# Expert weights in runs of 8 KB, experts finished in pairs, and the crowded path eight experts earlier, in a two-block transformer kernel

## The chip, the cores and the metric

The kernel runs on one core of a Trainium2 chip. The metric is the device time of one execution in microseconds. It was 1775.2 us as the median of three runs (1770.57 to 1777.78 us). The program has five engines with queues of their own: PE (TensorE), DVE (VectorE), ACT (ScalarE), POOL (GpSimd) and SP (SyncE, which here does nothing but issue DMAs). PE's weight loads are listed apart as PEld.

## The reference, cut to what matters

One layer of a first block (attention and HGRN mixers, then a mixture of experts), followed by two layers of a second block, over 256 tokens with 1024 features. The change is in the mixture of experts:

```python
def hier_moe(h, w_rg, b_rg, w_re, b_re, w_gate, w_up, w_down):
    t = h.reshape(B * S, D)                              # 256 x 1024
    ...                                                  # router: two of 32 experts per token
    y = jnp.zeros((B * S, D), jnp.float32)
    for e in range(N_EXPERTS):                           # 32
        hid = jax.nn.silu(t @ w_gate[e]) * (t @ w_up[e]) # w_gate, w_up: 1024 x 512
        y = y + ((hid * dense_w[:, e:e + 1]) @ w_down[e]).astype(jnp.float32)   # 512 x 1024
    return y.reshape(B, S, D).astype(h.dtype)

def first_block(x, ...):
    ...
    x = x + merged @ w_out[l]
    h = rmsnorm(x, g_ffn[l])
    x = x + hier_moe(h, ...)
```

All weights are fp32. One expert has 3 x 1024 x 512 x 4 bytes = 6.29 MB, all 32 have 201.3 MB, and each is read once.

## The kernel before, in words

The program is written in three stages, phase A (mixers and router), phase B (experts) and phase C (second block). A scheduler lays out each engine's instructions from the order of the code and of the data. Buffers come from pools with a fixed number of places. An instruction that writes a place waits until the last reader of what lay there is done, and every engine works through its own list in order, SP too.

**Phase A.** `split_w` cuts fp32 weights into a high and a low part (tiles `hi`, written by ACT, and `lo`, written by DVE, 5 places), and each product is three matmuls (lines 148 to 150). The residual x stands in `x_sb`. At the end, `ev_out` adds the output of `w_out` to x in `x_sb`, transposes it, and the router is worked out.

**Phase B.** For each expert at most CAP = 32 tokens are worked on; a path for more is behind a branch. For eight experts at a time `gather` makes the normalised tokens `xg`, feature major, by matmuls of `x_sb` with one-hot rows `OH` (line 831). Then for each expert e:

- `load_expert(e + 3)` issues the DMAs for the expert three ahead: gate and up weights in two halves (tiles `wgu` or `xgu`, two DMAs of 1024 KB each), down weights in two halves (`wdn` or `xdn`, one DMA of 1024 KB each). There are seven places for halves, so half h of the whole sequence takes the place of half h - 7, that is, the halves of three and a half experts are held. Feature 128 k + p is in partition p at place k, so one run of bytes in memory is 2 KB long in the gate and up weights and 4 KB in the down weights.
- PE makes the gate and up products of 32 tokens, four blocks of 128 hidden features side by side in four column groups of the array (line 922). ACT applies silu, DVE multiplies, PE transposes the 128 x 128 result (line 928), DVE copies it out as `hid`.
- PE multiplies it with the down weights (line 935), two halves of 512 features, each in four column groups, one for each quarter of the hidden features; ACT and DVE copy the two halves out as `part`.
- A matmul with `ohT` scatters these rows to the tokens of both token blocks, and sums the four quarters, in four PSUM accumulators `acc` (line 939). `ohT` is made by DVE and two PE transposes (lines 914 to 918).

At e = 24 stands `overflow()`, the path for crowded experts: it counts tokens per expert, all engines read the largest count, and a branch (line 856) skips the body when the count is not above 32. SP meets that branch after the loads of expert 26 and before those of expert 27. The body would write the tile `part` by DMA. After expert 31, DVE adds the accumulators to `x_sb` (line 947).

**Phase C.** Feed-forward sublayers, pooling and attention, with weight loads `fw` in runs of 1 KB (`ffn_w_in`) and 4 KB (`ffn_w_out`). They use the same rings of places as the experts' weights.

Of the kernel before, what the change touches and what calls it, by code (L numbers as in the profile page):

```python
# [37 lines left out]
def shape_constants():  # L38
# [22 lines left out]
    # pooling: trailing mean minus token, [token in, group, token out]; the first 16 tokens, which have  # L61
    # shorter windows, and what the tokens after a block boundary take from before it, apart
# [10 lines left out]
def tile_model(ctx: ExitStack, tc: tile.TileContext, io, out, dbg=None, stop_after=None):  # L73
# [68 lines left out]
    def row_rstd(tb, scr):  # L142
        ss = small(1, "ss")
        lead["act"] = act.activation(out=scr, in_=x_sb[:, tb], func=AF.Square, accum_out=ss)
        return rstd(ss, 1, 1.0 / D)
# [6 lines left out]
    def split_w(spl, w, lo=None):  # L152
        """w [128, a, b] fp32 (a*b <= 1024) as hi + lo"""
        a, b = w.shape[1], w.shape[2]
        hi = v2(spl.tile([P, 1024], F32R, tag="hi", name="hi")[:, :a * b], b)
        if lo is None:
            lo = spl.tile([P, 1024], F32R, tag="lo", name="lo", bufs=5)
        lo = v2(lo[:, :a * b], b)
        lead["hi"] = act.copy(out=hi, in_=w)  # L159
        lead["lo"] = dve.tensor_tensor(out=lo, in0=w, in1=f32(hi), op=ALU.subtract)  # L160
        return hi, lo

    def gemm_nat(spl, hs, w, evac, tag="g", sw=()):
        """out[t, n] = sum_k h[t, k] w[k, n];  hs[tb] = (hi, lo) [128, KT, 128], w a list of parts [128, k, N<=512],
        sw what is split of w's product before w"""
# [17 lines left out]
    def ada_steps(sl, what, new_ev, tag, new_w, nk, eng):  # L183
        """modulation vectors of sublayer sl, as a list of steps: "ab" the shift and the gain
        (1 + scale) * norm_g as feature columns, "gate" the residual gate over all partitions"""
# [4 lines left out]
        def row(c, h, k0):  # L190
            """rows k0 .. of the product of silu(c) with 512 columns, summed over partitions later"""
# [52 lines left out]
        for c, h in rows:  # L244
# [4 lines left out]
            elif last:  # L249
                # the sums of a row have the time of a step to arrive  # L250
# [50 lines left out]
    # first weights ahead of small loads  # L301
# [65 lines left out]
    # grouped-query attention  # L367
# [95 lines left out]
    # per-feature columns  # L463
# [22 lines left out]
    # HGRN projections, feature major  # L486
# [90 lines left out]
            # within chunks  # L577
# [13 lines left out]
            # k_state to token major, chunk outer products  # L591
# [43 lines left out]
    # gates  # L635
# [3 lines left out]
    sp.dma_start(out=br[:, 4:36], in_=io["b_router_expert"][0:1].to_broadcast([P, 32]))  # L639
    for gi, Gt_ in enumerate((GA, GB)):  # L640
# [7 lines left out]
    # branches  # L648
# [31 lines left out]
    dve.tensor_scalar(out=gcol, in0=gcol, scalar1=float(D) ** 0.5, scalar2=None, op0=ALU.mult)  # L680
    lead["wr"] = dve.tensor_tensor(out=wr, in0=wr, in1=gcol[:, :, None].to_broadcast([P, 8, 36]), op=ALU.mult)
# [11 lines left out]
    def first_max(v, n):  # L693
        """one-hot of the first maximum of each row of v [128, n], and the maximum"""
# [7 lines left out]
    def probs(v, mx, n):  # L702
        """exp(v - max) and the reciprocal of its sum"""
# [6 lines left out]
    def router(tb):  # L710
        """expert weights of the tokens of a block, and each token's place among its expert's tokens"""
# [40 lines left out]
    for h in range(2):  # L752
# [4 lines left out]
        def ev_out(tb, o, h=h):  # L757
            xs = x_sb[:, tb, 512 * h:512 * h + 512]
# [6 lines left out]
            act.copy(out=xT, in_=t)  # L765
            for k in range(4):
# [7 lines left out]
    for tb in range(2):  # L774
        dump(f"x1_{tb}", x_sb[:, tb])
# [12 lines left out]
    def load_expert(e):  # L788
        """halves of the weights in 4 + 3 places in turn; the last experts leave px free"""
# [26 lines left out]
    def one_hots(OH, e, i0, i1):  # L816
        """slots of the tokens of experts e + i0 .. e + i1 - 1, times the tokens' norm factors"""
# [5 lines left out]
    def gather(OH, xg, i0, i1):  # L823
        """the normalised tokens of these experts, feature major"""
# [755 lines left out]
```

## Time and profile before

| | |
|---|---|
| time, median of three runs | 1775.2 us |
| lowest and highest | 1770.57, 1777.78 us |
| profiled execution, first to last instruction | 1773.4 us |
| PE busy | 1630.4 us, 92% |
| DVE, ACT busy | 957.4 us (54%), 635.0 us (36%) |
| HBM read | 470.13 MB |
| DMA packets under 2 KB, under 8 KB, in all | 105336, 258808, 258930 |

The profiled execution has no time on record besides its span; the span lies inside the range of the three runs, 1.8 us under their median. A view by stretch lists, for a stretch of the span, each engine's busy time in us with the number of its instructions, the clock granted to TensorE as a share of full speed, the mean busy share of the 16 DMA engines (it can pass 1, since packets overlap), and the GB/s that they moved. A list in order of time gives the start in us, the duration in us, the engine (SPq is SP's queue), the line, the operation, the tiles written and read, and in brackets how long the engine had been idle and what ended that.

### The profile page before, as it was taken

How to read it: one execution, taken by the hardware profiler on the slowest of the kernel's cores; microseconds unless marked ns; L12 is line 12 of the kernel's file. 1: busy time of each engine (PE TensorE's matmuls, PEld its weight loads, DVE VectorE, ACT ScalarE, POOL GpSimd, SP SyncE). 2: the span in 40 equal slices, each digit the busy share in tenths (PEclk: the TensorE clock that was granted, in tenths of full speed). 3: DMA queues.
4: the chain of work that ended last, by engine and by line, in shares of the span. 5: the costliest groups of instructions: out<-in, count | busy, mean ns of one | idle time of the engine just before them, and what ended most of it. 6: DMA issues, size and time to landing. Idle time of an engine off the chain costs nothing.

```text
span 1773.4 us, 25626 instructions
## 1 busy us (share of the span) xinstructions
PE 1630.4 (92%) x10491; PEld 1205.5 (68%) x10491; DVE 957.4 (54%) x1653; ACT 635.0 (36%) x1054; POOL 48.1 (3%) x55
## 2 busy tenths in 40 slices
PE   6999998999888775989999989999999999999998
PEld 5865576434333332337999769997899867789997
DVE  6645664212112110127778666878687777765563
ACT  4754442101001000016434344435543365555341
POOL 3000000000000000000000000000000010000000
PEclk9999898999999887999999989999999999999999
DMA  7476476999999999997998458895798564465540
GB/s 246 157 263 244 166 274 248 336 394 394 393 393 393 394 394 343 393 384 250 322 321 270 135 181 275 286 308 180 257 302 285 177 225 154 155 214 200 181 154 24
DMA packets 258930, 472.90 MB, mean 267 GB/s; under 512 B 12568, under 2 KB 105336, under 8 KB 258808
## 3 DMA queue, kind: packets, MB, share of 16 engines
q1 hardware_dynamic: 258808, 471.21, 75.4%
q8 instruction: 85, 1.39, 0.3%
q14 instruction: 37, 0.30, 0.1%
HBM read 470.13 MB, written 1.05 MB: 266 GB/s over the span
## 4 chain that ended last, share of the span: by engine, by line
PE 53%; DVE 4%; issue 1%; ACT 1%; POOL 1%; DMA 1%; POOLq 0%; SPq 0%; ACTq 0%; DVEq 0%
PE ps_g L150 9%; PE ps_g L148 9%; PE ps_g L149 9%; PE ps_acc L148 5%; PE ps_acc L149 5%; PE ps_acc L150 5%; PE ps_acc L939 2%; PE ps_g L922 2%; PE ps_g L935 1%; POOL rs L137 1%; PE ps_m L1406 1%; PE ps_m L221 1%; DMA fw<-in_ffn_w_in_dram 1%; DVE flo L160 1%; PE ps_m L235 1%
## 5 line engine op out<-in xcount | busy, mean ns | idle before, releaser
L148 PE MATMUL ps_g<-hh,hi 128*128 128x256 f32 x1024 | 293.7, 287 | 0.0
L149 PE MATMUL ps_g<-hl,hi 128*128 128x256 f32 x1024 | 289.9, 283 | 0.0
L150 PE MATMUL ps_g<-hh,fl 128*128 128x256 f32 x1024 | 289.5, 283 | 0.0
L1065 DVE TENSOR_TENSOR fl<-fw,hi 128x1024 fp32r<-128x1024 f32 x176 | 211.4, 1220 | 43.0 <-ACT hi L1064 35.1
L1064 ACT CAST hi<-fw 128x1024 fp32r<-128x1024 f32 x176 | 176.6, 1045 | 118.3 <-PE ps_g L149 76.6
L149 PEld LDWEIGHTS ps_g<-hl,hi 128*128 128x128 f32 x1024 | 194.6, 190 | 3.6 <-issue 2.4
L148 PEld LDWEIGHTS ps_g<-hh,hi 128*128 128x128 f32 x1024 | 193.4, 189 | 2.9 <-issue 1.7
L150 PEld LDWEIGHTS ps_g<-hh,fl 128*128 128x128 f32 x1024 | 193.2, 189 | 0.7 <-issue 0.7
L206 DVE SCALAR_TENSOR_TENSOR ev<-ada,condp,ev 128x512 f32<-128x512 f32 x196 | 146.6, 748 | 4.4 <-DMA ada<-in_ada_w_dram 1.3
L939 PE MATMUL ps_acc<-part,ohT 128*128 128x512 f32 x256 | 122.9, 615 | 24.3 <-ACT part L937 23.7
L150 PE MATMUL ps_acc<-hi,hd 128*128 128x512 f32 x352 | 139.5, 399 | 0.0
L148 PE MATMUL ps_acc<-hi,hd 128*128 128x512 f32 x352 | 138.8, 397 | 0.5 <-ACT hd L1086 0.5
L149 PE MATMUL ps_acc<-fl,hd 128*128 128x512 f32 x352 | 138.7, 395 | 0.0
L160 DVE TENSOR_TENSOR fl<-fw,hi 128x1024 fp32r<-128x1024 f32 x88 | 104.9, 1220 | 19.7 <-ACT hi L159 19.3
L159 ACT CAST hi<-fw 128x1024 fp32r<-128x1024 f32 x88 | 88.6, 1046 | 71.0 <-PE ps_acc L150 69.6
L925 ACT ACTIVATE sg<-ps_g 128x128 f32<-128x128 f32 x32 | 8.9, 277 | 279.8 <-PE ps_g L922 279.8
L939 PEld LDWEIGHTS ps_acc<-part,ohT 128*128 128x128 f32 x256 | 46.0, 193 | 85.7 <-ACT part L937 40.1
L148 PE MATMUL ps_g<-hi,hh 128*128 128x512 f32 x240 | 98.5, 412 | 1.3 <-ACT hh L1010 1.1
L922 PE MATMUL ps_g<-wgu,xg 128*32 128x256 f32 x1280 | 87.7, 396 | 12.3 <-DMA wgu<-in_w_exp_up_dram 12.3
L150 PE MATMUL ps_g<-hi,hl 128*128 128x512 f32 x240 | 97.0, 405 | 0.0
L937 DVE COPY part<-ps_g 128x512 f32<-128x512 f32 x32 | 22.1, 692 | 137.1 <-PE ps_g L935 110.6
L149 PE MATMUL ps_g<-fl,hh 128*128 128x512 f32 x192 | 78.3, 409 | 1.2 <-DVE fl L1065 1.1
(402 smaller groups left out, 2743.2 us busy)
## 6 DMA issues: line engine op xcount, KB each, us to landing
fw<-in_ffn_w_in_dram SPq DMA_DIRECT2D x88, 1024.0 KB, 7.8
ada<-in_ada_w_dram SPq DMA_DIRECT2D x112, 512.0 KB, 5.2
fw<-in_ffn_w_out_dram SPq DMA_DIRECT2D x44, 1024.0 KB, 6.4
wgu<-in_w_exp_gate_dram SPq DMA_DIRECT2D x40, 1024.0 KB
wgu<-in_w_exp_up_dram SPq DMA_DIRECT2D x40, 1024.0 KB, 14.6
wdn<-in_w_exp_down_dram SPq DMA_DIRECT2D x40, 1024.0 KB, 14.1
xgu<-in_w_exp_gate_dram SPq DMA_DIRECT2D x24, 1024.0 KB, 12.9
xgu<-in_w_exp_up_dram SPq DMA_DIRECT2D x24, 1024.0 KB, 14.7
```

Of the source, the lines that this page charges most:

```text
L137: lead["gp"] = gp.tensor_tensor(out=r, in0=ms, in1=mhalf[:, :n], op=ALU.pow)
L148: pe.matmul(o, ah, bh, start=start, stop=False)
L149: pe.matmul(o, ah, bl, start=False, stop=False)
L150: pe.matmul(o, al, bh, start=False, stop=stop)
L159: lead["hi"] = act.copy(out=hi, in_=w)
L160: lead["lo"] = dve.tensor_tensor(out=lo, in0=w, in1=f32(hi), op=ALU.subtract)
L206: eng.scalar_tensor_tensor(out=o, in0=wk, scalar=ck, in1=o, op0=ALU.mult, op1=ALU.add)
L922: pe.matmul(up[32 * j:32 * j + 32], xg[:, k, s0:s0 + CAP], w[k // 4][:, k % 4, :, j * P:j * P + P], start=k == 0, stop=k == 7)
L937: (act.copy if h == 0 else dve.tensor_copy)(out=part[:, 512 * h:512 * h + 512], in_=o)
L939: pe.matmul(acc[tb][h], ohT[:, tb], part[:, 512 * h:512 * h + 512], start=e == 0, stop=e == NE - 1)
L1064: act.copy(out=hi, in_=w[:, k_])
L1065: dve.tensor_tensor(out=lo_[:, k_], in0=w[:, k_], in1=f32(hi), op=ALU.subtract)
```

## The change

Five things are changed together.

1. **Weights.** Feature 8 p + k is now in partition p at place k (4 p + k for the hidden features of the down weights), so each partition's share of a DMA is one run of 8 KB. Gate and up weights of a half stand one behind the other. The tokens' features have to stand in the same order, so `ev_out` writes, by a strided ACT copy, a second form of x, `x_sb`, with feature 8 i + j in column 128 j + i; the plain form is a new tile, `x_in`. The norm gain gets the same order (`gq`). The new tile's room comes from one place fewer for `lo` (4 for 5) and for `w2` (8 for 9).
2. **Pairs.** `up_gate` runs per expert; `down` and the scatter run per pair of experts, after the second one. The four column groups hold two experts with two halves each, and each adds two matmuls in PSUM. One set of scatter matmuls and one `ohT` serve a pair. The number of down matmuls is the same, that of scatter matmuls and of transposes for `ohT` is halved.
3. **Transposes.** The 128 x 128 transpose on PE and its copy become one DVE transpose by 32 x 32 blocks from SBUF to SBUF.
4. **Crowded path.** `overflow()` stands at expert 16.
5. **x.** It is added to the accumulators by four matmuls at expert 26 (`add_x`), and after the last expert ACT and DVE copy two accumulators each to `x_sb`, where DVE had added four.

```diff
-            lo = spl.tile([P, 1024], F32R, tag="lo", name="lo", bufs=5)
+            lo = spl.tile([P, 1024], F32R, tag="lo", name="lo", bufs=4)
...
-    NW2 = 9
+    NW2 = 8
...
         def ev_out(tb, o, h=h):
-            xs = x_sb[:, tb, 512 * h:512 * h + 512]
+            xs = x_in[:, tb, 512 * h:512 * h + 512]
...
             act.copy(out=xT, in_=t)
+            act.copy(out=x_sb[:, tb].rearrange("p (j i) -> p j i", j=8)[:, :, 64 * h:64 * h + 64],
+                     in_=xs.rearrange("p (i j) -> p j i", j=8))
...
-            w = place(q, "gu", 4096, wg).rearrange("p (k a n) -> p k a n", a=2, n=512)
+            w = place(q, "gu", 4096, wg).rearrange("p (a k n) -> p a k n", a=2, n=512)
             for a, nm in enumerate(("w_exp_gate", "w_exp_up")):
-                dst.append((q, w[:, :, a], io[nm][0, e].rearrange("(k p) n -> p k n", p=P)[:, 4 * q:4 * q + 4]))
+                dst.append((q, w[:, a], io[nm][0, e].rearrange("(p k) n -> p k n", k=8)[:, 4 * q:4 * q + 4]))
...
-            dst.append((q + 0.5 if e == 2 else 2, w, io["w_exp_down"][0, e].rearrange("(k p) n -> p k n", p=P)[:, 2 * q:2 * q + 2]))
+            dst.append((q + 0.5 if e == 2 else 2, w, io["w_exp_down"][0, e].rearrange("(p k) n -> p k n", k=4)[:, 2 * q:2 * q + 2]))
...
+    def up_gate(e):
...
+        act.activation(out=sg, in_=up[:, 0], func=AF.Silu)
+        sq = pb.tile([P, P], F32, tag="sq", name="sq", bufs=2)
+        dve.tensor_tensor(out=sq.rearrange("p (j i) -> p i j", j=4), in0=v2(sg, 4), in1=up[:, 1].rearrange("p (i j) -> p i j", j=4), op=ALU.mult)
+        hid = pb.tile([P, P], F32, tag="hid", name="hid", bufs=4)
+        dve.transpose(out=hid, in_=sq)
+        return hid
...
+    def down(e, hid, ohT):
+        wd = [wts.pop(e + i)[1] for i in range(2)]
+        part = pb.tile([P, D], F32, tag="part", name="part", bufs=1)
+        for h in range(2):
+            c_ = slice(512 * h, 512 * h + 512)
+            o = ps("g", 512)
+            for jj in range(2):
+                for i in range(2):
+                    for q in range(2):
+                        r_, j = 32 * (2 * i + q), 2 * q + jj
+                        pe.matmul(o[r_:r_ + 32], hid[i][:, 32 * j:32 * j + 32], wd[i][q][:, jj, c_],
+                                  start=jj == 0, stop=jj == 1)
+            (act.copy if h == 0 else dve.tensor_copy)(out=part[:, c_], in_=o)
+            for tb in range(2):
+                pe.matmul(acc[tb][h], ohT[:, tb], part[:, c_], start=e == 0, stop=e == NE - 2)
...
     for e in range(NE):
-        if e == 24:
+        if e == 16:
             overflow()
+        if e == 26:
+            add_x()
...
+        if e % 2 == 0:
+            hid = [up_gate(e)]
+        else:
+            hid.append(up_gate(e))
+            down(e - 1, hid, back_rows(e - 1))
...
-            dve.tensor_tensor(out=xs, in0=acc[tb][h], in1=xs, op=ALU.add)
+            (dve.tensor_copy if h else act.copy)(out=x_sb[:, tb, 512 * h:512 * h + 512], in_=acc[tb][h])
```

**PE, first two experts.** Before, in PE's list from the end of expert 0's gate and up products (`wgu_2427`) on; `wdn_2428` and `wdn_2429` are expert 0's down weights, `OH` to `128x224` is the gather for experts 1 to 7:

```order
L922 MATMUL ps_g_2570<-wgu_2427,xg_2522 32x256 x16
L928 MATMUL ps_t_2606<-K_65,sg_2603 128x128
L935 MATMUL ps_g_2611<-wdn_2428,hid_2608 32x512 x2
L935 MATMUL ps_g_2611<-wdn_2429,hid_2608 32x512 x2
L935 MATMUL ps_g_2619<-wdn_2428,hid_2608 32x512
L939 MATMUL ps_acc_2518<-part_2610,ohT_2568 128x512
L939 MATMUL ps_acc_2520<-part_2610,ohT_2568 128x512
L935 MATMUL ps_g_2619<-wdn_2428,hid_2608 32x512
L935 MATMUL ps_g_2619<-wdn_2429,hid_2608 32x512 x2
L831 MATMUL ps_g_2641<-OH_2498,x_sb_64 128x224 x3
```

The same place of the changed kernel; `wdn_2436` is now expert 0's first half of the down weights, `wgu_2444` and `wgu_2445` are expert 1's gate and up weights, and L840 is the gather:

```order
L918 MATMUL ps_g_2569<-wgu_2435,xg_2530 32x256 x16
L840 MATMUL ps_g_2622<-OH_2506,x_sb_64 128x224 x4
L840 MATMUL ps_t_2629<-OH_2506,x_sb_64 128x224 x4
L840 MATMUL ps_g_2636<-OH_2506,x_sb_64 128x224 x4
L840 MATMUL ps_t_2643<-OH_2506,x_sb_64 128x224 x4
L918 MATMUL ps_g_2660<-wgu_2444,xg_2530 32x256 x16
L918 MATMUL ps_g_2660<-wgu_2445,xg_2530 32x256 x16
L937 MATMUL ps_t_2699<-K_65,lw_2700 128x128
L937 MATMUL ps_t_2699<-K_65,lw_2704 128x128
L953 MATMUL ps_g_2711<-wdn_2436,hid_2606 32x512
```

The last read of expert 0's down weights has moved behind the gather for experts 1 to 7 and behind expert 1's gate and up products.

**PE, end of the expert stage.** The changed kernel's list from the first read of `wdn_4951` on, the last weights that are loaded (the second half of expert 31's down weights; `wdn_4950` is the first half, `wdn_4865` and `wdn_4866` are expert 30's):

```order
L953 MATMUL ps_g_5170<-wdn_4951,hid_5156 32x512
L953 MATMUL ps_g_5170<-wdn_4865,hid_5117 32x512
L953 MATMUL ps_g_5170<-wdn_4866,hid_5117 32x512
L953 MATMUL ps_g_5170<-wdn_4950,hid_5156 32x512
L953 MATMUL ps_g_5170<-wdn_4951,hid_5156 32x512
L953 MATMUL ps_g_5182<-wdn_4951,hid_5156 32x512
L953 MATMUL ps_g_5182<-wdn_4865,hid_5117 32x512
L957 MATMUL ps_acc_2526<-part_5169,ohT_5167 128x512
L957 MATMUL ps_acc_2528<-part_5169,ohT_5167 128x512
L953 MATMUL ps_g_5182<-wdn_4866,hid_5117 32x512
L953 MATMUL ps_g_5182<-wdn_4950,hid_5156 32x512
L953 MATMUL ps_g_5182<-wdn_4951,hid_5156 32x512
```

Two scatter matmuls follow. Before, eight down matmuls of expert 31 alone stood there with four scatter matmuls behind them; now ten of the pair's sixteen stand behind the read of the last weights to come.

**SP, the branch.** The changed kernel's list of SP around the branch of the crowded path; `wdn_3636` and `wdn_3637` are expert 18's down weights:

```order
L815 DMA wgu_3635<-in_w_exp_gate_dram 128x2048
L815 DMA wgu_3635<-in_w_exp_up_dram 128x2048
L815 DMA wdn_3636<-in_w_exp_down_dram 128x2048
L815 DMA wdn_3637<-in_w_exp_down_dram 128x2048
L864 TENSOR_LOAD cmi_3724
L865 COMPARE_AND_BRANCH
```

Before, the same two rows of the branch (lines 855 and 856) stood behind expert 26's loads. SP's loads keep their order by expert otherwise.

## Rows read from the trace of the kernel before

**Rows 1.** The page: span, and the slices of DMA share and GB/s

```profile
span 1773.4 us, 25626 instructions
...
DMA  7476476999999999997998458895798564465540
GB/s 246 157 263 244 166 274 248 336 394 394 393 393 393 394 394 343 393 384 250 322 321 270 135 181 275 286 308 180 257 302 285 177 225 154 155 214 200 181 154 24
```

**Rows 2.** By stretch: length, PE, PEld, DVE, ACT, POOL busy; clock, DMA share, GB/s

```profile
333.00:688.00 355.00, 290.33 (x2200) 124.96 (x2200) 58.21 (x172) 29.89 (x70) 0.00 (x0) 0.95 1.04 393
688.00:704.00 16.00, 3.75 (x7) 1.22 (x10) 0.00 (x0) 0.58 (x1) 0.00 (x0) 0.50 0.72 257
704.00:781.00 77.00, 70.44 (x554) 26.57 (x553) 13.22 (x36) 5.17 (x12) 0.00 (x0) 1.00 1.04 393
568.00:664.00 96.00, 71.19 (x486) 29.01 (x486) 12.00 (x32) 4.89 (x11) 0.00 (x0) 0.87 1.04 393
```

**Rows 3.** Same columns, three short stretches

```profile
412.00:417.00 5.00, 5.00 (x17) 2.89 (x16) 0.59 (x1) 0.42 (x1) 0.00 (x0) 1.00 1.05 387
403.00:407.00 4.00, 4.00 (x49) 1.91 (x51) 0.00 (x0) 0.00 (x0) 0.00 (x0) 1.00 1.02 408
784.00:793.00 9.00, 7.17 (x85) 3.17 (x78) 1.89 (x5) 0.86 (x2) 0.00 (x0) 1.00 1.10 348
```

**Rows 4.** SP's queue in the expert stage: start, us, line, DMA issued

```profile
319.70 0.37 SPq L806 DMA_DIRECT2D wdn<-in_w_exp_down_dram  x1
...
685.43 1.18 SPq L806 DMA_DIRECT2D xdn<-in_w_exp_down_dram  x1
699.86 0.38 SPq L806 DMA_DIRECT2D xgu<-in_w_exp_gate_dram  x1
...
768.29 2.56 SPq L806 DMA_DIRECT2D wdn<-in_w_exp_down_dram  x2
```

**Rows 5.** PE in the expert stage: start, us, line, operation, idle before it

```profile
345.80 0.33 PE L928 MATMUL ps_t<-K,sg 128*128 128x128 f32 x1 [0.71 <-DVE sg L926]
...
348.34 1.98 PE L939 MATMUL ps_acc<-part,ohT 128*128 128x512 f32 x4
...
358.44 0.33 PE L928 MATMUL ps_t<-K,sg 128*128 128x128 f32 x1 [0.71 <-DVE sg L926]
```

**Rows 6.** PE at the end of the expert stage, same columns

```profile
788.87 1.93 PE L935 MATMUL ps_g<-wdn,hid 128*32 128x512 f32 x16 [0.38 <-DVE hid L930]
791.53 3.70 PE L939 MATMUL ps_acc<-part,ohT 128*128 128x512 f32 x8 [0.72 <-ACT part L937]
...
801.75 0.79 PE L148 MATMUL ps_g<-hi,hh 128*128 128x512 f32 x1 [0.20 <-ACT hi L1064]
```

**Rows 7.** PE at its beginning, same columns

```profile
327.58 1.05 PE L922 MATMUL ps_g<-wgu,xg 128*32 128x256 f32 x10
...
330.08 2.36 PE L922 MATMUL ps_g<-wgu,xg 128*32 128x256 f32 x38
```

**Rows 8.** By stretch (columns of rows 2), two early stretches

```profile
308.00:313.00 5.00, 5.00 (x50) 2.15 (x50) 1.03 (x3) 0.07 (x1) 0.00 (x0) 0.65 0.23 52
330.00:333.00 3.00, 2.44 (x39) 1.19 (x38) 2.22 (x10) 0.28 (x1) 0.00 (x0) 1.00 0.25 44
```

**Rows 9.** What PE waited for, 310 to 842 us: total, times, longest

```profile
PE ps_acc L939 <- ACT part L937: 23.7, 11, 19.6
```

**Rows 10.** Line 856, the branch: durations in ns, first and last start; who waited

```profile
L856 SPq EVENT_SEMAPHORE  x8: 17/17/17, 690.5 to 699.5; - x8
...
  ACT part L937: 22.0, 1
```

**Rows 11.** Tile lo: what its engine sat idle for, and who waited for it

```profile
  PE ps_g L149: 18.0, 16
...
  PE ps_g L149: 1.6, 2
```

**Rows 12.** ACT before the expert stage: a copy of 512 columns

```profile
291.44 0.58 ACT L765 COPY xT<-ps_acc 128x512 f32<-128x512 f32 x1
```

More of the change, by code (lines that the diff above doesn't have):

```diff
@@ L143, in row_rstd @@
         ss = small(1, "ss")
-        lead["act"] = act.activation(out=scr, in_=x_sb[:, tb], func=AF.Square, accum_out=ss)
+        lead["act"] = act.activation(out=scr, in_=x_in[:, tb], func=AF.Square, accum_out=ss)
         return rstd(ss, 1, 1.0 / D)
@@ L639, in tile_model @@
     sp.dma_start(out=br[:, 4:36], in_=io["b_router_expert"][0:1].to_broadcast([P, 32]))
+    sp.dma_start(out=gq, in_=io["g_ffn"][0].rearrange("(p j) -> p j", j=8))
     for gi, Gt_ in enumerate((GA, GB)):
@@ L834, in gather @@
                 k = 2 * q + i
[L835 removed]
+                act.activation(out=xg[:, k, s_], in_=o[:, i], func=AF.Copy, scale=gq[:, k:k + 1])
     OH = new_oh()
@@ L893, in tile_model, with add_x @@
     xg = None
+    def add_x():
+        for tb in range(2):
+            for h in range(2):
+                pe.matmul(acc[tb][h], ident, x_sb[:, tb].rearrange("p (j i) -> p i j", j=8)[:, 64 * h:64 * h + 64],
+                          start=False, stop=False)
+    def up_gate(e):
+        w = wts[e][0]
+        s0 = (e % 8) * CAP
+        up = ps("g", 2, P)
+        for k in range(8):
+            for j in range(4):
+                pe.matmul(up[32 * j:32 * j + 32], xg[:, k, s0:s0 + CAP], w[k // 4][:, :, k % 4, j * P:j * P + P],
+                          start=k == 0, stop=k == 7)
+        sg = pb.tile([P, P], F32, tag="sg", name="sg", bufs=2)
+        act.activation(out=sg, in_=up[:, 0], func=AF.Silu)
[4 more added lines that the diff above has]
+        return hid
@@ new lines, in back_rows @@
+    def back_rows(e):
+        oT_ = ps("t", 2, P)
+        for tb in range(2):
+            lw = pb.tile([P, 2, 2, CAP], F32, tag="lw", name="lw", bufs=2)
+            for i in range(2):
+                dve.tensor_scalar(out=lw[:, i], in0=iota32[:, None, :].to_broadcast([P, 2, CAP]),
+                                  scalar1=posm[:, tb, e + i:e + i + 1], scalar2=dense[:, tb, e + i:e + i + 1],
+                                  op0=ALU.is_equal, op1=ALU.mult)
+            pe.transpose(oT_[:, tb], lw.rearrange("p a b s -> p (a b s)"), ident)
+        ohT = pb.tile([P, 2, P], F32, tag="ohT", name="ohT", bufs=2)
+        dve.tensor_copy(ohT, oT_)
+        return ohT
@@ L908, in tile_model @@
             load_expert(e + 3)
-        w, wd = wts.pop(e)
-        s0 = (e % 8) * CAP
-        oT_ = ps("t", 2, P)
-        for tb in range(2):
-            lw = pb.tile([P, 4, CAP], F32, tag="lw", name="lw", bufs=1)
-            dve.tensor_scalar(out=lw, in0=iota32[:, None, :].to_broadcast([P, 4, CAP]), scalar1=posm[:, tb, e:e + 1],
-                              scalar2=dense[:, tb, e:e + 1], op0=ALU.is_equal, op1=ALU.mult)
-            pe.transpose(oT_[:, tb], lw.rearrange("p a s -> p (a s)"), ident)
-        ohT = pb.tile([P, 2, P], F32, tag="ohT", name="ohT", bufs=2)
-        dve.tensor_copy(ohT, oT_)
-        up = ps("g", 2, P)
-        for k in range(8):
-            for j in range(4):
-                pe.matmul(up[32 * j:32 * j + 32], xg[:, k, s0:s0 + CAP], w[k // 4][:, k % 4, :, j * P:j * P + P],
-                          start=k == 0, stop=k == 7)
-        sg = pb.tile([P, P], F32, tag="sg", name="sg", bufs=2)
-        act.activation(out=sg, in_=up[:, 0], func=AF.Silu)
-        dve.tensor_tensor(out=sg, in0=sg, in1=up[:, 1], op=ALU.mult)
-        hp_ = ps("t", P)
-        pe.transpose(hp_, sg, ident)
-        hid = pb.tile([P, P], F32, tag="hid", name="hid", bufs=2)
-        dve.tensor_copy(hid, hp_)
-        part = pb.tile([P, D], F32, tag="part", name="part", bufs=1)
-        for h in range(2):
-            o = ps("g", 512)
-            for j in range(4):
-                pe.matmul(o[32 * j:32 * j + 32], hid[:, 32 * j:32 * j + 32], wd[j // 2][:, j % 2, 512 * h:512 * h + 512],
-                          start=True, stop=True)
-            (act.copy if h == 0 else dve.tensor_copy)(out=part[:, 512 * h:512 * h + 512], in_=o)
-            for tb in range(2):
-                pe.matmul(acc[tb][h], ohT[:, tb], part[:, 512 * h:512 * h + 512], start=e == 0, stop=e == NE - 1)
+        if e % 2 == 0:
[3 more added lines that the diff above has]
+            down(e - 1, hid, back_rows(e - 1))
         if e == 29:
```

24 lines of the change are left out of this document (14 added, 10 removed).

## The prediction

> **What bounds the kernel now.** I read the slices first. In slices 8 to 18 the DMA share stands at 9 and the rate, in eight of the eleven, at 393 or 394 GB/s [rows 1]: the expert stage, in which 201.3 MB of weights pass. Nowhere else is the rate so flat, and it is the only part in which the change removes much. By stretch, 333 to 688 us ran at 393 GB/s with PE busy 290 of 355 us, and 704 to 781 us at 393 again [rows 2]. Between them lies a hole: 257 GB/s over 16 us, 5.5 us of transfer time lost. So the transfers set the pace, but not all the way to the end. In PE's list one expert takes 358.44 - 345.80 = 12.64 us [rows 5], where its weights take 6.29 MB / 393 GB/s = 16.0 us. Yet from 704 us PE was busy 70 of 77 us at full clock [rows 2]. The reason is the branch. PE waited up to 19.6 us there for ACT's copy into part [rows 9], and ACT 22.0 us for SP at line 856 [rows 10]: the skipped body writes part by DMA, so the copy has to wait until SP is past it. SP came late to the branch, since its last load before it was issued only at 685.43 us, and needed until 699.86 us for the next [rows 4]. After that PE had a backlog that it could not work off in the seven experts left, so its last scatter ended at 791.53 + 3.70 = 795.2 us [rows 6], about 13.7 us after the experts' last bytes (near 781.5 us: at 784 the rate is that of the next stage's loads, 348 GB/s [rows 3]). Both chains must get shorter for the stage to end earlier.
>
> **Transfer rate.** The rows give the price of a run at three lengths. SP's loads go out in order, so a stretch can be matched to its loads: 2 KB runs (gate, up) moved at 387 GB/s, 4 KB runs (down) at 408, 1 KB runs (feed-forward, first stage) at 348 [rows 3]. On one of 16 DMA engines that is 84.7, 160.6 and 47.1 ns a run. One KB more costs 37.6 ns from 1 to 2 KB and 37.9 from 2 to 4 KB: a straight line with about 9.3 ns fixed per run. For 8 KB it gives 160.6 + 4 x 37.9 = 312 ns, an estimate of 420 GB/s. Lower bound: 8 KB no better than 4 KB, 408. Upper: no fixed cost at all, 434. I take 420, since three lengths lie on the line.
>
> From 333 us on, 355 x 393 + 16 x 257 + 77 x 393 = 173.9 MB passed. At 393 GB/s they take 442.5 us, at 420 414.0: **-28.5 us**.
>
> The Trainium skill ("DMA: Bandwidth & Descriptors", "Why small descriptors are slow (HBM only)") puts the fixed cost of a packet at some 3 cycles of a 32-byte beat, so four runs of 2 KB and one of 4 KB would be 399 cycles and one and a half runs of 8 KB 388.5, 2.6% less. By that the term would be an estimated -11.6 us. The rows show 9.3 ns a run, more than twice those 3 cycles at the page's 850 MHz, and I go by the rows.
>
> **The branch.** At expert 16 SP meets it after expert 18's loads. Before, SP spent its time inside the issue of loads, and ran only about 10 us (4 MB) ahead of the bytes: after 685.43 us the transfers went on for some 10 us and then ran dry. I read this as a queue that holds so many runs. With runs four times (gate, up) and twice (down) as long it holds nearly three times the bytes, so SP is then held by free places alone. It issues expert 18's last load when pair 14, 15 is done, with nearly three experts, 40 us, still to pass, and its 14.4 us at the branch [rows 4] are hidden. The hole goes: **-5.5 us**; it stays (0) if the queue holds bytes. PE's wait goes too: part is written next only after expert 17's products, 30 us on.
>
> **Pairs on PE.** Two experts took 25.3 us. One of two sets of scatter matmuls goes (1.98 us a half [rows 5], two such rows an expert, 4.0 us), two PE transposes with their waits and one pair for ohT go as well; 21 us at most remain, against 2 x 6.29 MB / 420 GB/s = 30 us of transfer. So PE has 9 us to spare per pair, which cover the new DVE transposes (no row shows one; even 2 us each would fit), the smaller ohT rows, and add_x (four scatter-like matmuls, 3.7 us [rows 6]). DVE was busy 58 of 355 us [rows 2]. All these are costed at nothing; if PE were the bound, each would count.
>
> **Places held longer.** Expert e's down weights are released only after e + 1's. First, at the start: SP waits in order, and expert 3's second down load needs expert 0's place. Before, it was issued at 319.70 us [rows 4]. Now it stands behind the gather and expert 1's products. Expert 1's products began at 327.58 us [rows 7]; without expert 0's down, scatter and transposes (8 us) ahead of them they begin at about 319.6. They take 4.2 us (without ohT's transposes [rows 7]), silu to transpose 1.4 us, and 13 of 16 down matmuls, at 2 x 1.93 us for all [rows 6], 3.1: release at 328 us. By then 24.1 MB are loaded and the queue has run dry at about 320. The other 177.2 MB start at 329.3 and take 421.9 us: last bytes at 751.2 us, where before it was 781.5. That is -30.3; the two terms above are -34.0, so the early hole costs **+3.7 us** net, as before there were holes too, at 308 and 330 [rows 8], of which the second goes. Later it is free: expert e + 3's second down load (e even) needs the pair's end, some 7 us after e + 1's bytes land, and the stream reaches it 27 us after.
>
> **The end.** From the last bytes: landing 1.5 us, ten of sixteen down matmuls 2.4, two copies with their gaps 1.8, scatter 3.7 [rows 6]: 9.4 us at full clock. PE now idles a third of the time; where it idled a quarter, the granted clock averaged 0.87 (a mix of 2.4 and 1.2 GHz) [rows 2]. At half clock the matmuls double: 15.5. I take 11 for 13.7: **-2.7 us**. The last four additions become four copies on two engines, of which one follows the last scatter either way: 0. From there to the first feed-forward matmul all is as before (6.5 us to 801.75 [rows 6]); its first weights, 4.2 MB at 348 GB/s, land by 763 us, before they are needed.
>
> **Phase A.** PE waited 1.6 us for lo, DVE 18.0 us for PE to free its places [rows 11]: with four places DVE starts later, but a split still ends before PE needs it. Four ACT copies of 0.58 us [rows 12] join the router's chain. Between 0 and +6; I take **+2 us**.
>
> **Sum.** 1773.4 - 28.5 - 5.5 + 3.7 - 2.7 + 2.0 = 1742.4 us for a profiled execution. The median lies 1.8 us over the profiled span, run to run differs by 7 us, so I say 1743.
>
> **Rivals.**
> *Runs of 8 KB are no faster than 4 KB.* For it: no row shows 8 KB. Against: the straight line. 177.2 MB at 408 GB/s take 434.3 us, 12.4 more: 1755 us. By the three cycles of the Trainium skill (the section named above) it would be an estimated 1760.
> *The branch's hole moves along.* If SP's lead is bounded in bytes, it arrives as late as before: +5.5 us, 1749; PE's backlog is gone before expert 31 then, 15 experts on.
> *Slower: the new places in memory are read worse.* Partitions were 2 or 4 KB apart in memory, now 16 KB, so all engines step at a power of two. The gain is gone when the stream takes 421.9 + 31 = 453 us, at 391 GB/s, about the rate now; at 375 it takes 472.5 us, 1794 us. Against: going from 2 to 4 KB apart, the rate rose as the run length says [rows 3]. The Trainium skill ("DMA: Bandwidth & Descriptors", "Latency and other measured facts") tells of lost rate at row pitches of 2 MiB and up and little at 512 KiB; no row here shows such a pitch.
> *Other:* phase A loses over 6 us, or PE's low clock makes it late.
>
> **Numbers.** Forecast 0.62; no gain past 4 KB 0.11, a gain by the Trainium skill's three cycles 0.04; moved hole 0.11; worse reading 0.07; other 0.05. The range reaches from 434 GB/s (13.6 us less: 1729) to the second case with a few us of phase A: 1764. A run of this kernel tells 0.5% (9 us) from no change: faster 0.90, same 0.03, slower 0.07.
>
> **What would show it.** Right: some 420 GB/s flat from 330 to 750 us, SP idle for places instead of inside its issues, no dip at expert 16, PE waiting for wgu and xgu from about 350 us on, last scatter near 762, first feed-forward matmul near 769. Wrong: a rate of 408 or less, holes once per pair, PE busy throughout, or an expert stage that starts late.

## The result, and the profile after

The changed kernel takes 1752.5 us (median of four runs, 1750.7 to 1755.5) where the kernel before takes 1775.4 (four runs too, one more than ahead of the prediction, 1770.6 to 1777.8): ratio 0.9875, 95% interval 0.9857 to 0.9892. The forecast was 1743 us, in a range of 1729 to 1764: faster as forecast, by 22.9 us and not 32. The profiled execution is 24.1 us shorter than that of before.

The page of the changed kernel, with the rows that answer to [rows 1]:

```profile
span 1749.3 us, 25202 instructions
...
DMA  6478475799999999997987467986798565466540
GB/s 199 135 245 295 169 271 213 299 419 420 420 421 377 417 420 421 420 390 266 330 286 259 157 206 252 311 265 209 257 309 282 168 207 178 142 211 216 177 150 25
```

The flat part stands at 420, with one dent (slice 13, 377). By stretch, with the columns of [rows 2]:

```profile
312.00:320.00 8.00, 8.00 (x72) 4.36 (x71) 0.00 (x0) 2.14 (x5) 0.00 (x0) 0.58 0.57 211
...
328.00:336.00 8.00, 8.00 (x72) 3.35 (x64) 3.65 (x17) 0.86 (x2) 0.00 (x0) 1.00 0.11 15
...
344.00:552.00 208.00, 155.72 (x1305) 69.63 (x1293) 29.98 (x103) 14.60 (x37) 0.00 (x0) 0.90 1.01 420
...
560.00:568.00 8.00, 0.79 (x1) 0.50 (x2) 0.00 (x0) 0.59 (x1) 0.00 (x0) 0.56 0.58 216
568.00:576.00 8.00, 7.57 (x46) 2.60 (x48) 0.69 (x1) 0.00 (x0) 0.00 (x0) 0.80 0.94 383
...
577.00:760.00 183.00, 135.84 (x1118) 56.56 (x1108) 20.64 (x63) 10.38 (x27) 0.00 (x0) 0.90 1.01 420
```

So 420 GB/s as forecast, and PE idle for a quarter of the time. But two holes, stretches in which the transfers fall behind, are left: an early one (328 to 336 us at 15 GB/s, and a part of 312 to 320), and one at 560 to 576, where (420 - 216) x 8 and (420 - 383) x 8 make 1.9 MB, 4.6 us of transfer. SP's queue (columns of [rows 4]) shows both from the other side:

```profile
301.71 0.33 SPq L815 DMA_DIRECT2D xgu<-in_w_exp_gate_dram  x1
...
334.34 0.33 SPq L815 DMA_DIRECT2D wdn<-in_w_exp_down_dram  x1
...
538.97 0.33 SPq L815 DMA_DIRECT2D wgu<-in_w_exp_gate_dram  x1
541.47 0.33 SPq L815 DMA_DIRECT2D wgu<-in_w_exp_up_dram  x1
543.99 2.82 SPq L815 DMA_DIRECT2D wdn<-in_w_exp_down_dram  x2
566.83 0.34 SPq L815 DMA_DIRECT2D wgu<-in_w_exp_gate_dram  x1
```

The first load that waits for the end of phase A is issued at 301.71 us; before it was 293.34. Expert 0's down place comes free at 334.34 (319.70 in [rows 4]). And SP issues nothing from 546.8 to 566.83 us. From 350 us on it issues one load of 1 MB every 2.5 us, and what it then waits for is an older load:

```profile
SPq L815 <- DMA wgu<-in_w_exp_gate_dram: 63.5, 30, 3.9
```

The branch, line 865 now, with the columns of [rows 10]:

```profile
L865 SPq EVENT_SEMAPHORE  x8: 17/17/17, 553.9 to 566.4; - x8
...
L865 SPq COMPARE_BRANCH  x1: 50/50/50, 547.5 to 547.5; - x1
...
  ACT part L955: 14.2, 1
```

PE now waits for weights, 65.8 us in the stage where before it was 21.8 (total, times, longest):

```profile
PE ps_g L918 <- DMA wgu<-in_w_exp_up_dram: 41.3, 10, 8.0
PE ps_g L918 <- DMA xgu<-in_w_exp_up_dram: 24.5, 7, 7.9
PE ps_acc L957 <- ACT part L955: 12.7, 5, 11.0
```

Before:

```profile
PE ps_g L922 <- DMA wgu<-in_w_exp_up_dram: 12.3, 5, 3.3
...
PE ps_g L922 <- DMA xgu<-in_w_exp_up_dram: 9.5, 4, 3.3
```

The end of the stage, to be held against [rows 6]; the second row is one of PE's weight loads (PEld):

```profile
764.68 4.47 PE L953 MATMUL ps_g<-wdn,hid 128*32 128x512 f32 x22 [0.81 <-DVE sq L923]
766.38 0.15 PEld L953 LDWEIGHTS ps_g<-wdn,hid 128*32 128x32 f32 x7 [0.36 <-DMA wdn<-in_w_exp_down_dram]
769.08 1.98 PE L957 MATMUL ps_acc<-part,ohT 128*128 128x512 f32 x4
770.99 1.06 PE L953 MATMUL ps_g<-wdn,hid 128*32 128x512 f32 x6
772.88 1.99 PE L957 MATMUL ps_acc<-part,ohT 128*128 128x512 f32 x4 [0.83 <-DVE part L955]
...
781.39 0.79 PE L148 MATMUL ps_g<-hi,hh 128*128 128x512 f32 x1 [0.21 <-ACT hi L1104]
```

The last bytes of the experts land near 763 us (423 GB/s up to 760, 377 in the next 8 us, some 350 after that, the rate of the 1 KB runs), but the last load is complete on all DMA engines only at 766.34 us, and PE waits for it until 766.38. The last scatter ends at 774.9, before it was 795.2; the first feed-forward matmul begins 20.4 us earlier. The other 3.7 us of the 24.1 arise in phase C, whose code is the same: about half in the pooling layer, where in 8 us the granted clock was 0.77 and before 0.56, and 1.5 us some 450 us later, where in 16 us it was 1.00 and before 0.92 and 0.87. In all kernels below phase C, counted from that matmul, takes 968 to 973 us, so medians and that matmul can differ by this much.

A loss stands at the very start of phase A. DVE (start, us, line, operation, idle before it):

```profile
15.42 0.14 DVE L135 TENSOR_SCALAR ms<-ss 128x1 f32<-128x1 f32 x1
26.73 0.17 DVE L686 TENSOR_SCALAR gq<-gq 128x8 f32<-128x8 f32 x1 [11.17 <-DMA gq<-in_g_ffn_dram]
26.81 1.42 DVE L356 SCALAR_TENSOR_TENSOR xn<-x_in,rs,W 128x512 f32<-128x512 f32 x2
```

The multiplication of the new `gq`, line 686, whose result is first read 283 us later (at 309.37 us), stands in DVE's list ahead of the norm of the second token block. Its data come with the last of the small loads, issued at 23.77 us. DVE waits 11.17 us for them and PE 8.86 us for DVE.

### The profile page after: what moved, and what is told of

It reads as the page before. It is cut to its first block, busy times and chain, and to the rows that moved or that the text cites. A ratio compares the mean times of both kernels' runs of the same rounds, so it can differ in the third digit from the quotient of the medians.

```text
span 1749.3 us, 25202 instructions
## 1 busy us (share of the span) xinstructions
PE 1569.7 (90%) x10307; PEld 1185.4 (68%) x10307; DVE 935.5 (53%) x1620; ACT 632.1 (36%) x1044; POOL 48.9 (3%) x55
## 4 chain that ended last, share of the span: by engine, by line
PE 50%; DMA 10%; DVE 4%; issue 1%; POOL 1%; ACT 1%; SPq 0%; POOLq 0%; DVEq 0%; ACTq 0%
PE ps_g L148 10%; PE ps_g L150 10%; PE ps_g L149 9%; DMA wgu<-in_w_exp_up_dram 5%; PE ps_acc L148 5%; PE ps_acc L150 5%; PE ps_acc L149 5%; DMA xdn<-in_w_exp_down_dram 2%; DMA xgu<-in_w_exp_up_dram 1%; DMA wdn<-in_w_exp_down_dram 1%; PE ps_g L953 1%; POOL rs L137 1%; PE ps_m L221 1%; PE ps_m L1446 1%; DVE rt L1057 1%
## 5 line engine op out<-in xcount | busy, mean ns | idle before, releaser
L918 PE MATMUL ps_g<-wgu,xg 128*32 128x256 f32 x1280 | 91.7, 426 | 41.3 <-DMA wgu<-in_w_exp_up_dram 41.3
L923 DVE TENSOR_TENSOR sq<-sg,ps_g 128x128 f32<-128x128 f32 x32 | 11.9, 373 | 197.1 <-ACT sg L921 197.1
L918 PEld LDWEIGHTS ps_g<-wgu,xg 128*32 128x32 f32 x1280 | 45.7, 121 | 88.0 <-issue 70.5
L953 PE MATMUL ps_g<-wdn,hid 128*32 128x512 f32 x320 | 90.2, 631 | 6.4 <-DVE sq L923 6.4
L957 PE MATMUL ps_acc<-part,ohT 128*128 128x512 f32 x128 | 65.2, 633 | 22.1 <-ACT part L955 12.7
## 6 DMA issues: line engine op xcount, KB each, us to landing
wgu<-in_w_exp_gate_dram SPq DMA_DIRECT2D x40, 1024.0 KB, 19.9
xgu<-in_w_exp_gate_dram SPq DMA_DIRECT2D x24, 1024.0 KB, 19.9
```

The costliest lines, as they stand in the source:

```text
L918: pe.matmul(up[32 * j:32 * j + 32], xg[:, k, s0:s0 + CAP], w[k // 4][:, :, k % 4, j * P:j * P + P], start=k == 0, stop=k == 7)
L953: pe.matmul(o[r_:r_ + 32], hid[i][:, 32 * j:32 * j + 32], wd[i][q][:, jj, c_], start=jj == 0, stop=jj == 1)
L957: pe.matmul(acc[tb][h], ohT[:, tb], part[:, c_], start=e == 0, stop=e == NE - 2)
```

## The experiments

All kernels are variants of the changed one, but for e4. "First load" is the first that waits for the end of phase A, "scatter" the end of the last one, "FFN" the first feed-forward matmul; times in us. Each ratio is to runs of before on the same chip (medians of 1774.6 to 1775.7).

| kernel | median | ratio to before, 95% | first load | scatter | FFN |
|---|---|---|---|---|---|
| before | 1775.4 | | 293.34 | 795.2 | 801.75 |
| changed | 1752.5 | 0.9857 to 0.9892 | 301.71 | 774.9 | 781.39 |
| e1 gq later | 1744.1 | 0.9811 to 0.9841 | 289.40 | 762.5 | 769.03 |
| e2 crowded path's loads on POOL | 1751.0 | 0.9847 to 0.9876 | 301.30 | 770.0 | 776.49 |
| e3 experts 0, 1 single | 1749.7 | 0.9834 to 0.9865 | 304.03 | 771.9 | 778.53 |
| e4 before, fewer places | 1768.7 | 0.9947 to 0.9977 | 285.79 | 786.7 | 793.22 |
| e5 runs of 2 and 4 KB | 1778.2 | 1.0011 to 1.0030 | 298.45 | 800.6 | 807.14 |
| e6 all single | 1748.8 | 0.9840 to 0.9870 | 301.65 | 768.1 | 774.64 |
| e7 e1, copies on POOL | 1737.3 | 0.9781 to 0.9808 | 286.15 | 759.4 | 765.93 |
| e8 e1, e2 and e3 | 1735.6 | 0.9765 to 0.9797 | 291.47 | 754.9 | 761.46 |
| e9 branch at 24 | 1753.8 | 0.9868 to 0.9898 | 301.37 | 774.2 | 780.73 |
| e10 e2, e6 and e7 | 1728.6 | 0.9722 to 0.9748 | 286.85 | 747.7 | 754.24 |
| e11 e2, e3 and e7 | 1730.7 | 0.9731 to 0.9758 | 287.11 | 750.5 | 757.00 |

**e1: gq multiplied later.**

```diff
-    dve.tensor_scalar(out=gq, in0=gq, scalar1=float(D) ** 0.5, scalar2=None, op0=ALU.mult)
     lead["wr"] = dve.tensor_tensor(out=wr, ...)
...
     with tc.issue_after(lead["wr"].ins):
+        dve.tensor_scalar(out=gq, in0=gq, scalar1=float(D) ** 0.5, scalar2=None, op0=ALU.mult)
```

> The changed kernel, with the multiplication of gq (line 686) placed behind that of wr in DVE's list. Theory: phase A ended 8.4 us later than before because DVE reaches that multiplication at 15.6 us and waits 11.17 us in front of it for the DMA of gq, with PE idle for 8.9 us; then DVE waits nowhere there, the first loads after phase A are issued near 293 us where the changed kernel issued them at 301.71, and the time is about 8 us less, 1744 us. Rival: phase A is longer through fewer places for lo and w2 and the copies into x_sb; then the wait only moves and the time stays at 1752, within 2 us.

The wait is gone: DVE goes on with the second token block at once.

```profile
15.69 1.42 DVE L356 SCALAR_TENSOR_TENSOR xn<-x_in,rs,W 128x512 f32<-128x512 f32 x2 [0.74 <-POOL rs L137]
```

The first load comes 12.3 us earlier, the first feed-forward matmul 12.4 us, the median 8.4 us (phase C took 971.2 us in this run's profile, in the changed kernel's 967.9). So this one instruction cost 12.3 us of phase A, more than the 8.4 us by which phase A had grown: something else in the change must have made phase A shorter.

**e4: the kernel before, with fewer places.**

```diff
-            lo = spl.tile([P, 1024], F32R, tag="lo", name="lo", bufs=5)
+            lo = spl.tile([P, 1024], F32R, tag="lo", name="lo", bufs=4)
...
-    NW2 = 9
+    NW2 = 8
```

> The kernel before, with four places for lo instead of five and eight for w2 instead of nine, and nothing else. Theory: both are nearly free (PE waited 1.6 us for lo), so 0 to 2 us: 1775 to 1777 us. Rival: they carry the 8 us by which phase A ended later, through DVE starting its splits late and the next weights' loads behind them: 1781 to 1784 us.

Neither: the kernel gets faster, by 5.9 us in the median and by 7.55 us at the first load. Fewer places for `lo` make the scheduler lay out phase A in another order (with `w2` alone changed PE's order is that of before, with `lo` alone that of e4). By stretch, first before, then e4:

```profile
200.00:210.00 10.00, 8.47 (x69) 6.15 (x68) 8.32 (x15) 6.48 (x8) 1.71 (x1) 0.96 0.61 211
210.00:220.00 10.00, 10.00 (x27) 3.80 (x27) 2.84 (x6) 1.05 (x1) 0.00 (x0) 0.50 0.56 211
220.00:230.00 10.00, 10.00 (x32) 6.64 (x31) 3.00 (x6) 1.50 (x3) 1.01 (x1) 0.69 0.55 200
```

```profile
200.00:210.00 10.00, 9.51 (x65) 4.59 (x64) 4.59 (x16) 0.15 (x1) 0.00 (x0) 1.00 0.31 107
210.00:220.00 10.00, 10.00 (x44) 7.53 (x44) 7.26 (x10) 5.95 (x7) 2.00 (x1) 1.00 0.70 257
```

Before, behind a stretch in which PE had gaps, it ran 10 us at 1.2 GHz and 10 us at a mean of 0.69: 8.1 us lost while it was busy throughout. In e4 it ran at 2.4 GHz there and lost 1.5 us (0.85 in 170 to 180 us). The difference of 6.6 us is most of the 7.55. By stretch the clock is known of one execution of each kernel only; that the gain is no accident of one execution is said by the medians (6 runs against 10) and by the clock granted over whole runs, 0.968 to 0.973 in e4's and 0.963 to 0.970 in those of before. The changed kernel and e1 have no such dip either (1.7 and 1.6 us lost).

**e7: the copies into x_sb on POOL**, on top of e1.

```diff
-            act.copy(out=x_sb[:, tb].rearrange("p (j i) -> p j i", j=8)[:, :, 64 * h:64 * h + 64],
+            gp.tensor_copy(out=x_sb[:, tb].rearrange("p (j i) -> p j i", j=8)[:, :, 64 * h:64 * h + 64],
```

> The changed kernel with gq multiplied behind wr, and the four copies into x_sb on POOL instead of ACT. Theory: the copies of 1.15 us on ACT stand in the router's chain and cost 3.6 us (first loads after phase A at 289.40 us with them, 285.79 in the kernel of before with the same number of places, which has none); on POOL, which is idle, they cost nothing: first loads near 286 us, and 3 to 4 us less than with gq late alone, 1741 us. Rival: POOL is so slow with them, or so much in DVE's way, that the router waits for x_sb or for its norm factor (POOL's power): 1744 us or more.

The first load comes 3.25 us earlier than in e1, the first feed-forward matmul 3.1 us. The median gains 6.8; the rest is phase C (968.2 us after 971.2). One line's instructions in the changed kernel and in e7 (durations in ns):

```profile
L772 ACT COPY x_sb<-x_in x4: 1151/1170/1195, 274.1 to 298.5; 128x512 f32<-128x512 f32 x4
```

```profile
L772 POOL COPY x_sb<-x_in x4: 1126/1158/1167, 261.1 to 282.6; 128x512 f32<-128x512 f32 x4
```

Such a copy, which reads every eighth feature, took 1.17 us; in e5, where it is plain, 0.61.

With e1 and e4 the 8.4 us of phase A part into -7.55 for fewer places, +12.3 for gq, and what is left between e1 and e4, 289.40 - 285.79 = +3.6. These three make 8.4 by their definition; that the rest is the copies is shown by e7, which takes 3.25 of it back.

**e2: the loads of the crowded path on POOL.** The path isn't taken; only who would issue its loads changes.

```diff
-                            sp.dma_start(out=wf_, in_=w_e[:, :, j * P:j * P + P])
+                            gp.dma_start(out=wf_, in_=w_e[:, :, j * P:j * P + P])
...
-                        sp.dma_start(out=wo_, in_=wd_e[:, j])
+                        gp.dma_start(out=wo_, in_=wd_e[:, j])
```

> The changed kernel, with the weight loads inside the crowded path (which is not taken) issued by POOL instead of SP. Theory: SP stands at the branch because the way past the body waits on all eight DMA semaphores, so until all that it has issued has landed; without loads of SP in the body it does not wait, the hole at 560 to 576 us (4.6 us of transfer) is gone, PE's 11.0 us for part are gone, and the time is about 4.6 us less, 1748 us. Rival: SP loses the 20 us to the jump itself (fetching instructions behind 8 MB of loads) or arrives too late with its lead of eight loads; then it still issues nothing for 19 us or more, and the time stays at 1752.

The hole is gone, and SP goes on without a pause:

```profile
560.00:568.00 8.00, 4.35 (x57) 1.90 (x55) 0.68 (x2) 0.28 (x1) 0.00 (x0) 0.94 1.02 420
568.00:576.00 8.00, 3.41 (x32) 1.61 (x32) 0.00 (x0) 0.00 (x0) 0.00 (x0) 0.63 1.01 417
```

```profile
543.40 2.81 SPq L815 DMA_DIRECT2D wdn<-in_w_exp_down_dram  x2
548.34 0.33 SPq L815 DMA_DIRECT2D wgu<-in_w_exp_gate_dram  x1
550.82 0.33 SPq L815 DMA_DIRECT2D wgu<-in_w_exp_up_dram  x1
```

So SP's jump takes no time to speak of. In the changed kernel's order of instructions the row behind the skipped body reads

```
L865 UNCONDITIONAL_BRANCH [waits DMAHW0_49,DMAHW1_49,DMAHW2_49,DMAHW3_49,DMAHW4_49,DMAHW5_49,DMAHW6_49,DMAHW7_49]
```

and in e2 it waits for none. These are the eight semaphores that SP's loads take in turn, each load waiting until the one eight before it has landed: a body with loads of SP makes it wait until all that it has issued has landed. In e2's trace SP has none of the eight EVENT_SEMAPHORE rows at that line, and its branch alone is left:

```profile
L865 SPq COMPARE_BRANCH  x1: 50/50/50, 546.9 to 546.9; - x1
```

PE's 11.0 us for `part` are gone too. The first feed-forward matmul comes 4.9 us earlier, the price of the hole. The median shows only 1.5 us of it: phase C took 973.0 us in this run's profile, with a clock of 0.51 in the 8 us of the pooling layer where the changed kernel had 0.77.

**e9: the crowded path at expert 24.**

```diff
-        if e == 16:
+        if e == 24:
```

> The changed kernel with the crowded path at expert 24, where it stood before. Theory: SP waits at the branch until all that it has issued has landed, wherever the branch stands, so the hole of 4.6 us stands at some 680 us instead of 560, and PE catches up in the seven experts behind it, since it has nine us to spare a pair: 1752 us, within 2 us. Rival, as the prediction had it for the kernel before: seven experts are too few for PE's backlog, and the last scatter comes later than 774.9 us: 1756 us or more.

```profile
680.00:688.00 8.00, 0.43 (x1) 0.43 (x2) 0.00 (x0) 0.58 (x1) 0.00 (x0) 0.50 0.46 190
688.00:696.00 8.00, 8.00 (x15) 2.12 (x15) 0.69 (x1) 0.00 (x0) 0.00 (x0) 0.64 0.98 377
704.00:760.00 56.00, 41.28 (x410) 18.21 (x402) 7.27 (x23) 2.56 (x7) 0.00 (x0) 0.91 1.01 420
```

The same hole (5.2 us), 120 us later, and the last scatter at 774.2 us: the place of the branch is worth nothing here, one part of the change without effect.

**e5: the old runs.** x, hidden features and the norm gain are put in the plain order to match.

```diff
-                dst.append((q, w[:, a], io[nm][0, e].rearrange("(p k) n -> p k n", k=8)[:, 4 * q:4 * q + 4]))
+                dst.append((q, w[:, a], io[nm][0, e].rearrange("(k p) n -> p k n", p=P)[:, 4 * q:4 * q + 4]))
```

> The changed kernel with the expert weights back in the order of before (runs of 2 KB in gate and up, 4 KB in down, x and hidden features in the plain order to match) and everything else as changed. Theory: the transfers set the pace of the stage and their gain is the run length alone: 177 MB at 393 instead of 420 GB/s take 29 us more, 1776 to 1783 us, as slow as the kernel before or slower, with 386 to 402 GB/s in the stage. Rival: pairs and fewer transposes carry a part of the gain; then 1762 to 1770 us.

```profile
344.00:568.00 224.00, 160.48 (x1285) 70.57 (x1282) 30.47 (x109) 14.88 (x38) 0.00 (x0) 0.88 1.04 394
```

394 GB/s again, with PE idle for over a quarter of the time, and the gain is gone: 25.7 us more than the changed kernel, also at the first feed-forward matmul (25.75). Its plain copies end phase A earlier, and expert 0's place comes free at 331.85 us and not 334.34; without that 28.2 us. Run length and the distance between partitions in memory change together here, so e5 can't tell them apart; for the length speaks that the rate lands on the line of [rows 3].

**e3: experts 0 and 1 single.** `down` and `back_rows` get a count n; a single expert's four quarters lie in the four column groups.

```diff
-        if e % 2 == 0:
+        if e < 2:
+            down(e, [up_gate(e)], back_rows(e, 1), 1)
+        elif e % 2 == 0:
             hid = [up_gate(e)]
```

> The changed kernel, with experts 0 and 1 down-projected and scattered one by one and pairs from expert 2 on. Theory: the transfers stand still at 328 to 336 us (15 GB/s) because expert 0's down place is released only at 334.34 us, after expert 1's products; singly it is released near 326 us, that hole of 7.7 us shrinks to about 2 us, and the time is 5 to 6 us less, 1747 us. Rival: another place is late next (the half that waits for the gather and for expert 1's products, or that of expert 1's down weights) and the hole only moves: 1751 to 1753 us.

```profile
320.00:328.00 8.00, 7.37 (x60) 3.59 (x53) 1.91 (x7) 1.65 (x4) 0.00 (x0) 0.95 0.80 299
328.00:336.00 8.00, 8.00 (x36) 5.42 (x35) 0.69 (x1) 1.57 (x4) 0.00 (x0) 1.00 0.86 322
```

The hole shrinks. But in this execution phase A, the same instructions in the same order, ended 2.3 us later (304.03), with a clock of 0.66 at 150 to 160 us and 0.86 in the next 10 us, where the changed kernel had 0.83 and full speed; so expert 0's place comes free at 330.07 us and not near 326. From the first load to the first feed-forward matmul 5.2 us are gained, as the theory had it, on the whole 2.9 us.

**e6: all experts single** (`if e < NE:` in the place of `if e < 2:`).

> The changed kernel with every expert down-projected and scattered by itself, in runs of 8 KB. Theory: PE has room (12.6 us an expert by the trace of before, 15.0 us of transfer), so pairs gain nothing in the middle and cost the early hole: 1748 to 1752 us, like the run in which only experts 0 and 1 are single (1749.7). Rival: PE becomes the bound, since its low clock and its wait at the branch use up the 2.4 us an expert that it has left: 1758 us or more, with the rate under 420 GB/s behind expert 16.

The first feed-forward matmul comes 6.75 us earlier, with phase A the same, and the median 3.7. So pairs, the largest rewrite in the change, cost time. PE's work is hidden by the transfers with them and without (156.02 of 183 us busy from 577 us on, at 419 GB/s).

**e8: e1, e2 and e3 together.**

> The changed kernel with gq multiplied behind wr, the loads of the crowded path on POOL's queue, and experts 0 and 1 done one by one. Theory: three separate losses ahead of and in the transfers, so they add: first feed-forward matmul at 781.39 - 12.4 - 4.9 - 2.9 = 761.2 us, and 1736 to 1739 us. Rival: with an earlier start of the stage the early hole has another cause (the places for gate and up weights, or PE at half clock), and the gains overlap: 1740 to 1743 us.

The first feed-forward matmul begins at 761.46 us, where the sum was 761.2, and the median is 1735.6: the three losses add.

**e10 and e11: the four repairs, single or in pairs.** Both have the loads of the crowded path and the copies on POOL and gq behind wr; in e10 all experts are single, in e11 only 0 and 1.

> The changed kernel with gq behind wr, the copies into x_sb on POOL, the loads of the crowded path on POOL's queue, and every expert single. Theory: the four gains add. From the first feed-forward matmul of the run with three fixes (761.46 us) the copies take 3 us, and experts one by one 4 us in the tail (in the run with all experts single the last scatter ended 3.8 us earlier against the last load than with pairs): 754.5 us, and 1727 to 1731 us. Rival: the 3.8 us came from PE's backlog, which kept its clock up; without the wait at the branch PE idles, its clock is 1.2 GHz at the end as with pairs, and single experts gain nothing: 1731 to 1735 us.

> The same as the run with four fixes, but experts 2 to 31 in pairs. Theory: PE has more idle time, its clock is low when the last bytes land, and two experts' down products and scatter follow them: first feed-forward matmul near 758.5 us, 1731 to 1735 us, so 3 to 4 us behind single experts. Rival: with no backlog in either, pairs and single experts end alike, within 1.5 us.

PE and its weight loads at the end, e10 and then e11:

```profile
741.73 0.18 PEld L953 LDWEIGHTS ps_g<-wdn,hid 128*32 128x32 f32 x7 [0.25 <-DMA wdn<-in_w_exp_down_dram]
...
744.01 3.70 PE L957 MATMUL ps_acc<-part,ohT 128*128 128x512 f32 x8 [0.36 <-ACT part L955]
```

```profile
741.99 0.16 PEld L953 LDWEIGHTS ps_g<-wdn,hid 128*32 128x32 f32 x8 [0.90 <-DMA wdn<-in_w_exp_down_dram]
...
748.49 1.98 PE L957 MATMUL ps_acc<-part,ohT 128*128 128x512 f32 x4 [0.83 <-DVE part L955]
```

The last down weights land at the same time in both. From there to the end of the last scatter e10 takes 747.71 - 741.73 = 6.0 us, e11 750.47 - 741.99 = 8.5: behind the last bytes a pair has two experts' down products to do, a single expert one. The low clock that was expected for e11 is not the cause: it was 1.00 there in both. The first feed-forward matmul is 2.8 us apart, the medians 2.1. e10, at 1728.6 us, beats both kernels: ratio to before 0.9735 (0.9722 to 0.9748).

## Why the prediction was right, and where not

The sum was 1742.4 us for a profiled execution; it took 1749.3. Step by step:

- **Transfer rate: right.** Forecast 420 GB/s from a straight line through three run lengths, measured 420, or 312 ns a run of 8 KB on one of 16 DMA engines; forecast -28.5 us, measured 28.2 (e5). The Trainium skill's three cycles a packet ("DMA: Bandwidth & Descriptors", "Why small descriptors are slow (HBM only)") gave an estimated -11.6 us; the runs decide for the fixed 9.3 ns of [rows 3].
- **The branch: the step that failed.** The prediction read SP's late arrival as a queue that holds so many runs, and had SP with long runs "held by free places alone", 40 us ahead, its time at the branch hidden. The first half fits the runs, though none tests it: with the short runs of e5 the issue of one load lasted up to 7.06 us, with 8 KB 0.33. But behind that limit stands the next: SP has at most eight loads in flight, 8 MB or 20 us (19.9 us from issue to the last step of a load's semaphore, median, for gate, up and down loads alike), and at the branch it waits for all eight, so any lead is spent there. The eight waits stood in [rows 10], and what they wait for was not asked. The hole went from 5.5 to 4.6 us: -0.9 and not -5.5. That is the rival of the hole that moves along, with its price about right (5.5 for 4.6) and another cause. PE's wait stayed as well (11.0 us), but PE had caught up by the end, as that rival said.
- **Pairs on PE: right at nothing** in the middle: PE has idle time and waits for weights. The DVE transposes took 0.31 us each; they and `add_x` were not run by themselves. What was not asked is whether the old way would have been hidden too. It is (e6).
- **Places held longer: right in kind.** Forecast release 328 us; measured 334.34, of which 8.4 are phase A's. From the first load to the last bytes the stage took 461.3 us after 488.2: -26.9 = -28.2 - 0.9 + 2.2, so the early hole cost, by difference, 2.2 where +3.7 were forecast.
- **The end: right in size, partly by luck.** 774.9 - 763 = 11.9 us, forecast 11, before 13.7. The 11 was a choice between 9.4 at full clock and 15.5 at half. The clock was 1.00 from 762.4 us to the end of the scatter, so it cost nothing; what cost was the landing, 3.3 us from 763 to 766.3 where 1.5 was forecast, and from there 8.5 us passed where the other terms make 7.9.
- **Phase A: a mis-sized term.** Forecast +2 us, between 0 and +6; measured +8.4, the sum of three parts that were each wrong. Fewer places were taken as a small loss and gave 7.55 us; the copies were priced by a plain copy [rows 12] and take twice that, on the router's chain (3.6 us are left for them, of which e7 took back 3.25); and the multiplication of gq was not seen. It could have been read ahead of the run: in DVE's list it is the ninth instruction, ahead of the second token block's norm, and its load is the last of the small ones.

So 1742.4 + 6.4 (phase A) + 4.6 (branch) - 1.5 (early hole) + 0.9 (end) + 0.3 (rate) = 1753.1, and 3.7 us less of phase C give 1749.4, the profile's 1749.3. As the early hole is a difference, the sum closes by itself. That the forecast is not further off is partly luck: it had no term for what phase C gave back.

Of the signs named, the flat 420 GB/s and PE's waits for weights came. The dip at expert 16 stayed, SP waits for older loads and not for places, and the last scatter ended at 774.9 us and not near 762.

What stays open is phase C's part in the medians: 968 to 973 us for the same instructions. The trace shows a lower clock in the pooling layer, but not what decides it from kernel to kernel.

## What to carry to other kernels

Ask of each new instruction, however small, where the scheduler puts it in its engine's list and when its data land: one multiplication of 0.17 us cost nearly half of what the longer runs gained. A branch whose body holds loads of an engine made that engine wait here for all its loads at the skip; put them on a queue that has nothing in flight, as e2 did with POOL's. If transfers set the pace, a rewrite that only saves work on another engine gains nothing, and what it delays (places, the work behind the last bytes) is paid for, here with 6.75 us (e6).

## What the runs showed of the hardware

A larger buffer count isn't safely faster: four places for `lo` instead of five took 5.9 us off, in the profiled executions mostly because TensorE's clock did not fall to 1.2 GHz in a stretch of 16 us. An ACT copy of 512 columns that reads every eighth element took 1.17 us where the plain one took 0.61. PE needed 6.1 us for the jump over the skipped body (its COMPARE_BRANCH in the changed kernel, 6.4 us before) where SP's took 0.05 us.
